# One inference step of an attention and convolution hybrid: SP's transfers in the attention in the kernel's order, and conv sums dealt later

## The chip, the cores and the metric

The kernel runs on one core of a Trainium2 chip. The metric is the device time of one execution in microseconds (us), the median of several runs. Five engines run at the same time, each with its own list of instructions: TensorE (PE, matmuls, with its weight loads shown as PEld), VectorE (DVE), ScalarE (ACT), GpSimd (POOL) and SyncE (SP). SP issues nearly all DMA transfers here. An instruction that waits for another engine or for a transfer holds up whatever stands behind it in the list of its own engine.

## What is computed

One layer of a streaming encoder, for a prompt of 1024 frames and a sample of 32 frames that continues 512 cached ones. The model width is 1024, with 16 heads of 64 channels and a causal depthwise convolution of width 31. The reference, cut to what matters:

```python
def mixer_inputs(x, norm_g, w_in, b_f, q_g, k_g):
    h = rmsnorm(x, norm_g)
    cols = lambda a, w: h @ w_in[:, a:a + w]
    q = rmsnorm(cols(OFF_Q, ATTN_WIDTH).reshape(B, T, N_HEADS, HEAD_DIM), q_g) * (HEAD_DIM ** -0.5)
    k = rmsnorm(cols(OFF_K, ATTN_WIDTH).reshape(B, T, N_HEADS, HEAD_DIM), k_g)
    v = cols(OFF_V, ATTN_WIDTH).reshape(B, T, N_HEADS, HEAD_DIM)
    logf = jax.nn.log_sigmoid((cols(OFF_F, N_HEADS) + b_f).astype(jnp.float32))
    u = cols(OFF_UA, CONV_WIDTH) * jax.nn.sigmoid(cols(OFF_UB, CONV_WIDTH))
    ga, gb, ma, mb = (cols(o, 1024) for o in (OFF_GA, OFF_GB, OFF_MA, OFF_MB))
    return q, k, v, logf, ga, u, gb, ma, mb

def fox_attend(q, k, v, cq, ck, qpos, kpos):
    s = einsum('bqhd,bkhd->bhqk', q, k) + (cq - ck)       # cumulative log forget gates
    p = softmax(where(qpos >= kpos, s, min))
    return einsum('bhqk,bkhd->bqhd', p, v)

def mixer_outputs(x, o_attn, conv, ga, gb, ma, mb, ln_g, ln_b, w_pa, w_pb, w_out):
    ya = (o_attn * silu(ga)) @ w_pa
    yb = (silu(layernorm(conv, ln_g, ln_b)) * silu(gb)) @ w_pb
    return x + (sigmoid(ma) * ya + sigmoid(mb) * yb) @ w_out
```

All products are made in float32 accuracy: a weight and an activation are each split into a high and a low part, and three matmuls (high by high, low by high, high by low) stand for one.

## The kernel before

**Stages.** By the trace: the inputs are transposed and the first convolution input is made (to about 55 us); u and v projections follow (to about 210); then q and k, two feature blocks of 128 channels at a time, with the convolution's taps on DVE (to about 530); the gate ga (to about 580); the attention (to about 1087); and the closing projections pa, pb and out.

**A projection** (`steps`) takes one 128-channel feature block: one `raw` weight tile of 512 KB is loaded (L109), ACT reads it once for its scale (`junk`, L117) and makes the high part (`wh`, L138), DVE makes the low part (`wl`, L141), and PE goes over three chunks of 352 columns, each of eight steps of three matmuls (L183). A finished chunk is read out of PSUM by ACT (`t`, L926) and stored by SP (`s_gb` and the like, L927).

**The attention** has 16 heads of 8 query blocks and four blocks of sample heads. The list `seq` holds them in order; iteration n of the main loop does this:

```python
start(seq[n + 3])                                   # scores of a block, L1087 and L1088
if getattr(seq[n + 5], "i", 1) == 0:
    seq[n + 5].head.load()                          # eight transfers, L942 to L949
b.turn()                                            # transposes of block n, L1112
fill(4)                                             # 12 matmuls of a gate projection, L183
seq[n - 2].values()                                 # for block 7: 40 matmuls po, L1131
heads[...].load_v()                                 # V of the next head, L956
```

`head.load()` brings QB, KB, QA and KA of one head, six pieces of 256 KB and two of 16 KB, 1568 KB in all. The first scores matmul (L1087) reads KB and QB, the second (L1088) KA and QA. The pool `hp` has two buffers of each, so one head can be read while another is loaded. The gate projections gb, ma and mb serve as filler: `fill(4)` takes four steps of them, half a chunk, so a chunk spans two iterations. The filler's PSUM comes from one bank (`pq`). The output of a pair of heads is stored from `ot` (L1140) after two steps on DVE (L1136, L1138).

**What sets the order.** A scheduler orders each engine's instructions ahead of the run. In the attention PE is taken out of it (`tc.manual_schedule(engines={E.PE})`): PE runs in the order in which the kernel is written. SP, DVE, ACT and POOL are ordered by the scheduler, so that a transfer written late in the program can stand early in SP's list.

**Convolution.** `conv_taps(f)` puts 31 taps of filter f in the list `taps`: the first is an ACT instruction that makes y (L361), the others are DVE instructions (L364). `beat`, called once for each projection step, deals them out at the rate of the stage. After the taps follow `from_shift` and `into_sums` (L341 to L347), which add y to `mean` on DVE, square y on ACT (L342) and add the squares to `rstd` on POOL (L347). `later(n, fn)` calls fn n steps later. In the q/k stage POOL also makes the low part of squares for the norm statistics (`sql`, L863), which PE multiplies (`pst`, L871). `u_tile` clears the first 30 columns of a convolution input (L388).

Of the kernel before, what the change touches and what calls it, by code (L numbers as in the profile page):

```python
# [8 lines left out]
F32 = mybir.dt.float32  # L9
# [4 lines left out]
AF = mybir.ActivationFunctionType  # L14
# [15 lines left out]
CW = T + 30 + TS  # L30
# [23 lines left out]
def build(tc, xT, xt, wv, wf, ckT, cv, clT, stT, vec, cst, yT, kT, vO, lfO, cpT, csT):  # L54
    nc = tc.nc
# [3 lines left out]
    def pool(name, bufs=1, stack=es, **kw):  # L59
        return stack.enter_context(tc.tile_pool(name=name, bufs=bufs, reuse_waits="tile", **kw))  # L60
# [19 lines left out]
    rstd = lnp.tile([128, TT], F32, name="rstd")  # L80
# [108 lines left out]
    late = []  # L189
# [3 lines left out]
    def later(n, fn):  # L193

        pace["n"] += 1
        late.append((pace["tick"] + n, pace["n"], fn))
        late.sort(key=lambda e: e[:2])
# [82 lines left out]
    class Banks:  # L280

        n = 0
# [11 lines left out]
    cvp = pool("cvp", 2, stack=pcv)  # L294
    us = {}
    taps = []
    pend = []

    def pump(n):
        for _ in range(min(n, len(taps))):  # L300
            taps.pop(0)()

    PCS = ((0, T, 0), (T + 30, TS, T))
    sides = {}
# [22 lines left out]
    def kept(f, y):  # L327
        nc.sync.dma_start(s_y[f, :, :T], y[:, :T])
        nc.sync.dma_start(s_y[f, :, T:], y[:, T + 30:])
# [6 lines left out]
    def into_sums(f, y):  # L336
        for o, n, a in PCS:
            if f == 0:
                nc.vector.tensor_copy(mean[:, a:a + n], y[:, o:o + n])
            else:  # L340
                nc.vector.tensor_add(mean[:, a:a + n], mean[:, a:a + n], y[:, o:o + n])  # L341
        nc.scalar.activation(y, y, AF.Square)  # L342
        for o, n, a in PCS:
            if f == 0:
                nc.gpsimd.tensor_copy(rstd[:, a:a + n], y[:, o:o + n])
            else:
                nc.gpsimd.tensor_add(rstd[:, a:a + n], rstd[:, a:a + n], y[:, o:o + n])  # L347
        if f == 7:
            sides["ready"] = True

    def sums(f):
        return [lambda: from_shift(f, sides["y", f]), lambda: into_sums(f, sides["y", f])]

    def conv_taps(f):
        u = us.pop(f)

        def tap(i):
            w = vec_t[:, V_WDW + f * KC + i:V_WDW + f * KC + i + 1]
            if i == 0:
                y = sides["y", f] = (u7p if f > 5 else cvp).tile([128, CW], F32, name="y", tag="y", bufs=2)  # L360
                nc.scalar.activation(y, u[:, 0:CW], AF.Identity, bias=vcol(V_BDW, f), scale=w)  # L361
                return 0.1
            y = sides["y", f]
            t = nc.vector.scalar_tensor_tensor(y, u[:, i:i + CW], w, y, op0=ALU.mult, op1=ALU.add)  # L364
            if f > 5:
                tc.keep_in_program_order(t)
            if i == KC - 1:
                kept(f, y)

        items = [lambda i=i: tap(i) for i in range(KC)]  # L370
        if f == 7:
            taps.extend(pend + items)
            pend.clear()
        else:
            taps.extend(items[:4] + pend + items[4:])
            pend[:] = sums(f) if f else []

    def pieces(o, n):
# [5 lines left out]
    def u_tile(f):  # L384
        if f > 3:
            pump(len(taps) - 97)
        u = us[f] = (u7p if f > 5 else cvp).tile([128, UW], F32, name="u", tag="u", bufs=2 if f > 5 else 4)
        nc.gpsimd.memset(u[:, 0:30], 0.0)  # L388
        nc.sync.dma_start(u[:, 30 + T:60 + T], stT[f])
        return u  # L390

    def u_done(f):
        u = us[f]
        nc.sync.dma_start(cpT[f], u[:, T:T + 30])
        nc.sync.dma_start(csT[f], u[:, 62 + T:62 + T + 30])
        conv_taps(f)

    def u_steps(f, pj):
        u = u_tile(f)

        def ev_ub(c, sl, ps, inv):
            for a, b in pieces(c * CH, CH):
                nc.scalar.mul(u[:, b], ps[:, a], inv)
            if c == 2:
                for b in (slice(30, 30 + T), slice(60 + T, 60 + T + TS)):
                    sides["sigmoid"] = nc.scalar.activation(u[:, b], u[:, b], AF.Sigmoid)

        def ev_ua(c, sl, ps, inv):
            for a, b in pieces(c * CH, CH):
                nc.vector.scalar_tensor_tensor(u[:, b], ps[:, a], inv, u[:, b], op0=ALU.mult, op1=ALU.mult)  # L410

        for g, ev in (("ub", ev_ub), ("ua", ev_ua)):
            for _ in steps((g, f), X, XL, pj, ev):
                yield
        u_done(f)

    def u_proj(*a, **k):
        for _ in u_steps(*a, **k):
            pass
# [14 lines left out]
    E = mybir.EngineType  # L434
# [40 lines left out]
    def vcol(base, f):  # L475
        return vec_t[:, base + f:base + f + 1]
# [64 lines left out]
    def x_split(c, ws, u, jobs):  # L541
# [21 lines left out]
        for kt in range(KT):  # L563
# [12 lines left out]
            drain((2, 5 if c == 0 else 2))  # L576

    u0 = u_tile(0)
    ua0 = xip.tile([128, TT], F32, name="ua0")
    ws0 = [[xip.tile([128, KT, 128], F16, name=a, tag=a, bufs=2) for a in ("wh0", "wl0")] for _ in range(2)]  # L580
# [96 lines left out]
    u7p = pool("u7p", 1, stack=p2, side="right")  # L677
# [52 lines left out]
    for c in range(4):  # L730
# [16 lines left out]
        for t in range(8):  # L747
            ps = pj.tile([128, 512], F32, name="pjv", tag="pj")
            n = 0
# [148 lines left out]
    def tables_again(last="sigmoid"):  # L898

        t = nc.scalar.preload_act_table_set(LNEXP)  # L900
        tc.add_manual_dep(t.ins, sides[last].ins.name,
                          mybir.DependencyInfo(mybir.DependencyClass.NoSync, mybir.DependencyReason.DATA),
                          reason="tables behind another's")
        sides["tables"] = t
# [52 lines left out]

    pace["rate"] = R_U
    u_proj(7, pj)
    assert not late  # L960
    pqk.close()
    pv.close()
    hp = pool("hp", 2, stack=p2, side="right")
# [6 lines left out]
            pass  # L970
    tables_again("silu")
    pump(len(taps) - (2 * KC - 2))
    order.close()
    pcv.close()
    pps.close()


    pe = ExitStack()
    pe.enter_context(tc.manual_schedule(engines={E.PE}))
    pace["rate"], pace["credit"] = R_A, 0.0  # L980
    taps.extend(sums(7))
    psS = pool("psS", 2, stack=p2, space=PS)
# [242 lines left out]
    for _ in flow:  # L1225
        pass
    p2.close()


    p3 = ExitStack()  # L1230
# [5 lines left out]
    class Banks3:  # L1236
        n = 0
# [383 lines left out]
```

## Time and profile before

| what | value |
|---|---|
| time, median of 3 runs | 1381.76 us (1381.34 to 1382.31) |
| time of the profiled execution | 1380.92 us |
| its span | 1379.1 us, mean granted clock of PE 0.988 |
| PE busy | 1327.1 us, 96% of the span, 9383 matmuls |
| DVE busy | 969.3 us, 70% |
| ACT busy | 722.4 us, 52% |
| POOL busy | 501.1 us, 36% |
| share of the chain of waits that ended last | PE 78%, DVE 7%, DMA 5%, ACT 4%, issue 4% |
| transferred | 194.96 MB, mean 141 GB/s |

The busy time of an engine is the time in which it worked; the span is from the first to the last instruction. The chain of waits is followed back from the last instruction to what released each step. "Issue" is time in which an engine waited for nothing that the profile shows. In rows of SP's queue (SPq) the duration is that of the issue, not of the transfer. A wait row reads: engine, line, what it waited for, total us, times, longest us.

### The profile page before, as it was taken

To read this page: it belongs to the slowest core of one execution; us is meant where nothing else is said; L and a number is where in the kernel's file an instruction comes from. 1 tells how busy PE (TensorE), PEld (TensorE's weight loads), DVE (VectorE), ACT (ScalarE), POOL (GpSimd) and SP (SyncE) were. 2 spreads that over 40 slices of the span, in tenths; PEclk is the share of its full clock that TensorE was granted. 3 is DMA by queue.
4 is the path that set the end of the run, shared out by engine and by line. 5 is a ranking of instruction groups with operands and counts; after the bars stand their busy time and mean duration, and the time that the engine had idled before them with its cause. 6 is when DMAs were issued, how large, how long until landed. Compare 5 with 4: busy or idle time off the path is not lost.

```text
span 1379.1 us, 24809 instructions
## 1 busy us (share of the span) xinstructions
PE 1327.1 (96%) x9383; PEld 1008.5 (73%) x9383; DVE 969.3 (70%) x1524; ACT 722.4 (52%) x1362; POOL 501.1 (36%) x556
## 2 busy tenths in 40 slices
PE   8999999999999999979889999989899999999999
PEld 5577876665666666657667667767676699999998
DVE  5797879777888888877768767645554479265664
ACT  6644555756676743555555556555554466333320
POOL 1101015445385820233423332222222239355553
PEclk8999999999999999999999999999999999999999
DMA  6333243429252533434445446544432498634462
GB/s 245 95 129 109 91 110 119 130 88 269 68 190 70 180 100 122 148 104 113 140 127 158 115 139 173 139 114 136 137 96 74 160 334 261 205 121 140 143 196 68
DMA packets 113496, 194.96 MB, mean 141 GB/s; under 512 B 34081, under 2 KB 80033, under 8 KB 113377
## 3 DMA queue, kind: packets, MB, share of 16 engines
q1 hardware_dynamic: 113232, 193.31, 45.8%
q8 instruction: 74, 1.21, 0.4%
q14 instruction: 46, 0.37, 0.1%
q10 hardware_dynamic: 144, 0.07, 0.0%
HBM read 127.68 MB, written 65.64 MB: 140 GB/s over the span
## 4 chain that ended last, share of the span: by engine, by line
PE 78%; DVE 7%; DMA 5%; ACT 4%; issue 4%; POOL 1%; SPq 1%; ACTq 0%; DVEq 0%; POOLq 0%
PE pj L183 53%; PE pjv L754 6%; PE pj L1453 5%; PE po L1131 5%; DMA raw<-wf 4%; PE ptr L1112 3%; PE psS L1087 2%; PE psS L1088 2%; DVE y L364 2%; DVE nm L1092 2%; DVE wl L141 1%; ACT P L1095 1%; ACT t L926 1%; PE pst L871 1%; POOL sql L863 1%
## 5 line engine op out<-in xcount | busy, mean ns | idle before, releaser
L183 PE MATMUL pj<-xh,wh 128*128 128x352 f16 (+2 forms) x1536 | 485.4, 316 | 18.7 <-ACT t L926 18.1
L183 PE MATMUL pj<-xl,wh 128*128 128x352 f16 (+2 forms) x1536 | 484.9, 316 | 0.5
L183 PE MATMUL pj<-xh,wl 128*128 128x352 f16 (+2 forms) x1536 | 484.8, 316 | 0.0
L183 PEld LDWEIGHTS <-wh 128*128 128x128 f16 x3072 | 303.2, 99 | 162.4 <-issue 3.7
L364 DVE SCALAR_TENSOR_TENSOR y<-u,vec_t,y 128x1086 f32<-128x1086 f32 x240 | 341.8, 1424 | 17.3 <-ACT y L361 14.4
L1098 POOL TENSOR_SCALAR P<-P,nm 128x128 f32<-128x128 f32 (+7 forms) x128 | 124.1, 971 | 269.8 <-DVE nm L1097 239.3
L183 PEld LDWEIGHTS <-wl 128*128 128x128 f16 x1536 | 151.7, 99 | 93.4 <-issue 22.8
L141 DVE SCALAR_TENSOR_TENSOR wl<-raw,sc,wh 128x384 f16<-128x384 f32 (+1 forms) x192 | 117.4, 647 | 30.1 <-ACT wh L138 30.0
L1095 ACT ACTIVATE P<-psS,nm 128x128 f32<-128x128 f32 (+7 forms) x128 | 94.7, 740 | 74.3 <-DVE nm L1092 64.3
L1092 DVE TENSOR_REDUCE nm<-psS 128x1 f32<-128x128 f32 (+7 forms) x128 | 96.3, 754 | 7.1
L1115 ACT COPY pt<-ptr 128x512 f32<-128x512 f32 (+3 forms) x128 | 64.3, 502 | 59.3 <-PE ptr L1112 58.6
L1087 PE MATMUL psS<-KB,QB 128*128 128x256 f32 (+2 forms) x192 | 82.8, 432 | 11.4 <-ACT P L1095 11.3
L175 POOL TENSOR_TENSOR wl<-raw,wh 128x384 fp32r<-128x384 f32 (+1 forms) x51 | 63.1, 1264 | 73.9 <-ACT wh L172 58.0
L1112 PE MATMUL ptr<-ident,P 128*128 128x128 f32 x576 | 85.5, 275 | 0.0
L117 ACT ACTIVATE junk<-raw 128x1024 bf16<-128x1024 f32 x62 | 65.2, 1051 | 32.6 <-DMA raw<-wf 32.5
L863 POOL TENSOR_TENSOR sql<-sqf,sqh 128x352 fp32r<-128x352 f32 x48 | 61.6, 1284 | 54.6 <-ACT sqh L860 54.6
L138 ACT ACTIVATE wh<-raw,sc 128x1024 f16<-128x1024 f32 (+1 forms) x68 | 72.4, 1089 | 8.6 <-DVE sc L158 8.2
L1112 PEld LDWEIGHTS ptr<-ident,P 128*128 128x128 f32 x576 | 70.3, 142 | 5.8
L1131 PE MATMUL po<-pt,V 128*64 128x256 f32 x640 | 72.6, 382 | 1.3 <-ACT pt L1115 1.3
L1097 DVE RECIPROCAL nm<-nm 128x1 f32<-128x1 f32 x128 | 20.5, 160 | 73.8 <-ACT P L1095 72.8
L1090 DVE TENSOR_TENSOR psS<-psS,cmask 128x128 f32<-128x128 f32 x128 | 37.5, 294 | 49.2 <-PE psS L1088 48.4
L754 PE MATMUL pjv<-vwh,xh 128*128 128x260 f16 x256 | 70.1, 274 | 0.0
(271 smaller groups left out, 2584.7 us busy)
## 6 DMA issues: line engine op xcount, KB each, us to landing
raw<-wf SPq DMA_DIRECT2D x92, 512.0 KB
QB<-s_q SPq DMA_DIRECT2D x32, 256.0 KB
KB<-s_k SPq DMA_DIRECT2D x32, 256.0 KB
kT<-qn SPq DMA_DIRECT2D x8, 528.0 KB
s_ga<-t SPq DMA_DIRECT2D x24, 176.0 KB
s_gb<-t SPq DMA_DIRECT2D x24, 176.0 KB
s_ma<-t SPq DMA_DIRECT2D x24, 176.0 KB
s_mb<-t SPq DMA_DIRECT2D x24, 176.0 KB
```

Of the source, the lines that this page charges most:

```text
L138: nc.scalar.mul(wh[:, ks, :], raw[:, ks, :], self.s[:, i:i + 1])
L141: nc.vector.scalar_tensor_tensor(wl[:, ks, :], raw[:, ks, :], self.s[:, i:i + 1], wh[:, ks, :], op0=ALU.mult, op1=ALU.subtract)
L183: nc.tensor.matmul(ps, a[:, kt, :], b(kt, sl), start=(first and n == 0), stop=(last and n == N - 1))
L364: t = nc.vector.scalar_tensor_tensor(y, u[:, i:i + CW], w, y, op0=ALU.mult, op1=ALU.add)
L754: nc.tensor.matmul(ps[:, :VC], a, b, start=(n == 0), stop=(n == 23))
L863: nc.gpsimd.tensor_sub(sql, sqf, f32(sqh))
L1087: nc.tensor.matmul(ps[:, b, :wm], QB[:, qsl], KB[:, ksl], start=True, stop=False)
L1092: nc.vector.tensor_reduce(nm[:, 0:1], ps[:, :nb, :w], axis=AX.XY, op=ALU.max, negate=True)
L1095: nc.scalar.activation(P[:, :nk].rearrange("p (b w) -> p b w", b=nb), ps[:, :nb, :w], AF.Exp, bias=nm[:, 0:1], accum_out=nm[:, 1:2])
L1098: nc.gpsimd.tensor_scalar(P[:, :nk], P[:, :nk], nm[:, 2:3], 1.0, op0=ALU.mult, op1=ALU.mult)
L1112: nc.tensor.transpose(pt[:, 128 * j:128 * j + 128], P[:, 128 * (4 * u + j):128 * (4 * u + j) + 128], ident)
L1131: nc.tensor.matmul(po[rows], V[:, j, :], parts[c][:, j, :], start=(c % 2 == 0 and j < 2), stop=(c % 2 == 1 and j >= 2 * c))
```

## The change

Five edits. In the attention SP joins PE in `manual_schedule`, so that SP issues its transfers in the order in which the kernel is written; behind the attention's loop that region ends and a new one with PE alone begins. In `into_sums` the square is dealt 9 steps later and the additions on POOL 13 steps later. The first tap of filters 0 to 5 is put five places before the end of the list of the taps that still stand, y gets a third buffer there, and the pending sums follow three taps instead of four. The clearing of u goes from POOL to DVE. What is still due in `late` is done at the end of the ga stage, where before it had to be empty ahead of it.

```diff
-        nc.scalar.activation(y, y, AF.Square)
-        for o, n, a in PCS:
-            if f == 0:
-                nc.gpsimd.tensor_copy(rstd[:, a:a + n], y[:, o:o + n])
-            else:
-                nc.gpsimd.tensor_add(rstd[:, a:a + n], rstd[:, a:a + n], y[:, o:o + n])
-        if f == 7:
-            sides["ready"] = True
+
+        def added():
+            for o, n, a in PCS:
+                if f == 0:
+                    nc.gpsimd.tensor_copy(rstd[:, a:a + n], y[:, o:o + n])
+                else:
+                    nc.gpsimd.tensor_add(rstd[:, a:a + n], rstd[:, a:a + n], y[:, o:o + n])
+            if f == 7:
+                sides["ready"] = True
+
+        later(9, lambda: nc.scalar.activation(y, y, AF.Square))
+        later(13, added)
...
-                y = sides["y", f] = (u7p if f > 5 else cvp).tile([128, CW], F32, name="y", tag="y", bufs=2)
+                y = sides["y", f] = (u7p if f > 5 else cvp).tile([128, CW], F32, name="y", tag="y", bufs=2 if f > 5 else 3)
...
         items = [lambda i=i: tap(i) for i in range(KC)]
+        if f < 6:
+            taps.insert(max(0, len(taps) - 5), items.pop(0))
...
-            taps.extend(items[:4] + pend + items[4:])
+            taps.extend(items[:3] + pend + items[3:])
...
-        nc.gpsimd.memset(u[:, 0:30], 0.0)
+        nc.vector.memset(u[:, 0:30], 0.0)
...
-    assert not late
...
+    while late:
+        late.pop(0)[2]()
...
-    pe.enter_context(tc.manual_schedule(engines={E.PE}))
+    pe.enter_context(tc.manual_schedule(engines={E.PE, E.SP}))
...
+    pe.close()
+    pe = ExitStack()
+    pe.enter_context(tc.manual_schedule(engines={E.PE}))
```

Line numbers of the changed kernel are larger by 6 from the conv edits on, and by 7 from the attention's loop on.

**SP early in the attention, before.** The list of SP around the loads of heads 2 (`QB_7326` to `KA_7327`) and 3 (`QB_7677` and on); `t_...` are the chunks of a gate projection in the order in which they are made.

```order
L946 DMA QA_7325<-s_q_57 64x1024
L947 DMA QA_7325<-s_aq_61 4x1024
L927 DMA s_gb_67<-t_7066 128x352
L948 DMA KA_7327<-s_k_58 64x1024
L949 DMA KA_7327<-s_ak_62 4x1024
L109 DMA raw_7423<-wf 128x1024
L109 DMA raw_7513<-wf 128x1024
L927 DMA s_gb_67<-t_7143 128x352
L927 DMA s_gb_67<-t_7212 128x352
L1009 DMA vc_7690<-cv 128x4x256
L956 DMA V_7276<-s_v_59 128x8x64
L927 DMA s_gb_67<-t_7310 128x352
```

The loads of head 2 stand ahead of three stores of the filler, two raw tiles directly behind them.

**The same place in the change.**

```order
L933 DMA s_gb_67<-t_7143 128x352
L933 DMA s_gb_67<-t_7212 128x352
L962 DMA V_7276<-s_v_59 128x8x64
L933 DMA s_gb_67<-t_7310 128x352
L948 DMA QB_7326<-s_q_57 64x1024
L949 DMA QB_7326<-s_q_57 64x1024
L950 DMA KB_7328<-s_k_58 64x1024
L951 DMA KB_7328<-s_k_58 64x1024
L952 DMA QA_7325<-s_q_57 64x1024
L953 DMA QA_7325<-s_aq_61 4x1024
L954 DMA KA_7327<-s_k_58 64x1024
L955 DMA KA_7327<-s_ak_62 4x1024
```

Head 2's eight loads now follow the stores of three chunks (t_7143, t_7212, t_7310) that they preceded; the raw tiles have moved behind the next stores, one at a time. PE's list is the same but for a few matmuls of the layernorm's sums.

**SP at head 5 of the change**, where the store of a pair's output and V stand ahead of the loads.

```order
L1127 DMA ga_8282<-s_ga_66 128x1024
L933 DMA s_gb_67<-t_8347 128x352
L1147 DMA s_o_70<-ot_7398 128x1024
L962 DMA V_8379<-s_v_59 128x8x64
L948 DMA QB_8427<-s_q_57 64x1024
L949 DMA QB_8427<-s_q_57 64x1024
L950 DMA KB_8429<-s_k_58 64x1024
```

In the list of before, the same `QB_8427` stood ahead of the store of chunk `t_8203`, several stores earlier.

## The prediction

> **What bounds the kernel now.** I read the busy shares first, then the time by stage, then PE's waits in the stage that the change touches, then SP's queue there.
>
> ```profile
> PE 1327.1 (96%) x9383; PEld 1008.5 (73%) x9383; DVE 969.3 (70%) x1524; ACT 722.4 (52%) x1362; POOL 501.1 (36%) x556
> 1087.00:1379.00 292.00, 288.06 (x1976) 279.64 (x1972) 176.74 (x227) 111.40 (x149) 149.69 (x120) 1.00 0.58 188
> 580.00:1087.00 507.00, 473.90 (x3463) 341.18 (x3463) 324.17 (x699) 273.11 (x589) 148.66 (x216) 0.98 0.45 124
> 210.00:530.00 320.00, 313.62 (x2073) 205.87 (x2072) 263.47 (x320) 205.88 (x369) 169.08 (x160) 0.99 0.43 134
> ```
>
> The first row is busy time, share and instructions. The others hold start and end, length, then the busy time of PE, its weight loads, DVE, ACT and POOL, the granted clock, the DMA share and GB/s. PE sets the end everywhere. After the attention (second row) it is solid, and nothing there can be won or lost by this change. In the attention (580 to 1087) PE is idle for 33 us, and a clock of 0.98 over 507 us costs some 8 to 10 us more. In the q/k stage (210 to 530) 6 us are idle. So a change of order gains at most some 50 us in all, while a PE that begins to wait loses without such a limit.
>
> ```profile
> PE pj L183 <- ACT t L926: 17.5, 17, 4.2
> PE psS L1087 <- ACT P L1095: 9.5, 5, 5.0
> ACT junk L117 <- DMA raw<-wf: 30.1, 14, 4.6
> 615.91 0.69 PE L1087 MATMUL psS<-KB,QB 128*128 128x384 f32 x1 [4.96 <-ACT P L1095]
> 607.15 0.50 SPq L949 DMA_DIRECT2D KA<-s_ak  x1
> 607.75 6.14 DMA raw<-wf
> ```
>
> These are waits in the attention (total, times, longest), one PE instruction with the idle time before it, one issue on SP, and one piece of the chain of waits. PE waits for ACT, ACT stands at a weight load that has not landed: at 615.91 the long stall is a raw tile issued at 607.75 that takes 6.14 us. It was issued directly behind the last (607.15) of a head's eight loads.
>
> ```profile
> 631.20 0.44 PE L1087 MATMUL psS<-KB,QB 128*128 128x384 f32 x1
> 634.02 0.48 PE L1087 MATMUL psS<-KB,QB 128*128 128x448 f32 x1
> 635.44 0.33 SPq L927 DMA_DIRECT2D s_gb<-t  x1
> 638.14 0.47 SPq L942 DMA_DIRECT2D QB<-s_q  x1
> 640.40 0.40 PE L1087 MATMUL psS<-KB,QB 128*128 128x256 f32 x1
> 640.64 0.28 PE L1088 MATMUL psS<-KA,QA 68*128 68x256 f32 x1
> SPq L942 <- PE psS L1088: 42.0, 13, 6.5
> SPq L927 <- ACT t L926: 115.0, 30, 8.9
> ```
>
> Here are PE's and SP's timeline around one change of head, and two of SP's own waits. At 640.40 PE starts block 0 of head 2; the QB that SP issues at 638.14 is already head 3's, one head ahead. SP waits in its queue 42.0 us for the old head's last scores and 115.0 us for results to store, and nobody pays, since loads are a whole head early.
>
> **The change: SP in the program's order.** In program order a head's loads (L942 to L949) stand behind the scores of the iteration that begins at S = 634.02, and block 0 of that very head comes two iterations later: KB and QB are used 640.40 - 634.02 = 6.4 us after S, KA and QA 6.6 us after S. So the lead shrinks from a head to two iterations, for all 15 heads after the first. What else SP must do first is what stands ahead of QB in its queue, and how long the loads take is in these rows:
>
> ```profile
> 735.01 0.45 SPq L942 DMA_DIRECT2D QB<-s_q  x1
> 737.29 0.59 SPq L945 DMA_DIRECT2D KB<-s_k  x1
> 739.10 0.45 SPq L948 DMA_DIRECT2D KA<-s_k  x1
> 739.58 0.48 SPq L949 DMA_DIRECT2D KA<-s_ak  x1
> 739.10 5.31 DMA KA<-s_k
> 765.09 4.15 DMA KB<-s_k
> DMA packets 788, 2.00 MB, mean 200 GB/s; under 512 B 138, under 2 KB 385, under 8 KB 787
> ```
>
> The loads were issued from 735.01, the last large one landed at 739.10 + 5.31 = 744.41, 9.4 us after the first issue, and a last small one is issued 0.48 us later; I take 9.65. That is 1568 KB, and the window from 735 to 745 moves 2.00 MB at 200 GB/s, so it is close to what the queue gives here.
>
> Head by head, by the new SP order:
> - Eight heads (1, 2, 3, 8, 12 to 15) have a store of a gate chunk ahead of QB, whose matmuls end only at S. By the rows at 635.44 the store leaves at S + 1.4 and takes 0.33, so QB leaves at S + 1.75, KA and QA are there at S + 11.4, and PE waits 11.4 - 6.6 = 4.8 us. 8 x 4.8 = 38.
> - Four heads (5, 7, 9, 11) have the store of a head pair's output and V ahead instead.
>
> ```profile
> 654.58 4.47 PE po L1131 x40
> 659.09 0.37 SPq L956 DMA_DIRECT2D V<-s_v  x1
> 665.72 0.32 SPq L1140 DMA_DIRECT2D s_o<-ot  x1
> ```
>
> The matmuls of the output end at 659.05, which is one iteration ahead of S (2.8 us, as from 631.20 to 634.02), and the store left 6.7 us after them. If it is ready before S, QB leaves 0.7 us after S at the latest and the wait is 0.7 + 9.65 - 6.6 = 3.7; if it takes 6.7 us again, 7.6. DVE made it late in the row at 665.72 behind other work, so I stay nearer the low end: 5. 4 x 5 = 20.
> - Three heads (4, 6, 10) have only stores whose chunk ended an iteration earlier: QB leaves at S, the wait is 3.0. Together 9.
>
> That is 67 us of new waiting. The other loads (V, ga, the sample's) stand where they have several iterations to land, and I cost them at nothing; without that cover the four samples would pay about the 2.0 us that PE now waits at one of them at worst, 8 in all.
>
> **The clock behind each wait.**
>
> ```profile
> 808.14 0.31 PE L183 MATMUL pj<-xh,wh 128*128 128x352 f16 x1 [2.15 <-ACT t L926]
> 807.40:810.90 3.50, 2.76 (x13) 1.77 (x13) 3.34 (x8) 1.47 (x5) 1.32 (x1) 0.74 0.14 52
> 810.90:812.50 1.60, 1.60 (x7) 0.66 (x6) 1.25 (x4) 1.16 (x3) 1.03 (x1) 0.50 0.00 0
> 618.00:621.40 3.40, 3.40 (x14) 1.93 (x14) 2.08 (x4) 1.06 (x3) 1.81 (x2) 0.50 0.00 0
> 621.40:625.00 3.60, 3.60 (x25) 2.76 (x24) 1.66 (x4) 1.53 (x4) 0.52 (x2) 1.00 0.02 5
> ```
>
> After the 2.15 us of idle at 808.14 the granted clock falls to 0.50 until 812.50, and after the 5 us at 615.91 a whole stretch of 3.4 us runs at 0.50 and then at 1.00 again. A stretch of 3.4 us at half speed loses 1.7 us. I count it for 14 of the 15 heads: 24 us. The Trainium skill, "TensorE: Matmul & The Clock Gate", section on the HAM clock gate, has the clock fall only after an idle window of about 3.4 us; the row at 808.14 differs, with 2.15 us of idle. By the skill's figure the 24 us would shrink to little, which is the second rival below.
>
> **What the same edit gives back.** In the new order a raw tile's load no longer stands in a pair behind a head's eight, and with PE waiting at each head ACT catches up. I take all of the 17.5 + 9.5 = 27 us of PE's waits for ACT above as gone, and the 8 us of low clock behind them. Between nothing and 37 us, I take 35, near the top, because 30.1 us of ACT's waits are for raw alone.
>
> **The conv edits.** In the q/k stage the square and the additions of a conv sum block others:
>
> ```profile
> 327.20 2.84 POOL L347 TENSOR_TENSOR rstd<-rstd,y 128x1024 f32<-128x1024 f32 x2 [2.40 <-ACT y L342]
> 330.98 0.46 PE L871 MATMUL pst<-sql,bones 128*128 128x352 f32 x1 [2.43 <-POOL sql L863]
> PE pst L871 <- POOL sql L863: 5.9, 4, 2.4
> L388 POOL MEMSET u<- x8: 123/123/124, 0.9 to 188.6; 128x30 f32 x8
> ```
>
> POOL stands 2.40 us at its addition for ACT's square, then works 2.84 us, and PE's statistics matmul at 330.98 waits 2.43 us for the product queued behind. Dealt some steps later, the addition finds its input ready: I take 2.4 us plus 1.7 of clock and a little of the rest, 5 us gained. The bound above is all 5.9 and twice the clock, 9; the bound below, that the 2.84 us of addition now hit another product at each of seven filters, is 7 x 2.4 = 17 lost. Eight clearings of 0.12 us moved from POOL to DVE, the third y buffer and the drained rest lie beside PE's work: nothing, at most 1 us.
>
> **The sum**: 67 + 24 - 35 - 5 = +51 on the profiled 1380.92, hence 1432; the median of the runs shown is 0.8 us higher than that execution: **1433 us**.
>
> **Rivals.**
> - *The clock holds.* Each head's wait is split in two: KB's last half is issued 2.3 us after QB (735.01, 737.29) and lands some 4.15 to 5.3 us later, at S + 8.2 to 9.3, so the first scores matmul (L1087) runs between two idle pieces of 1.8 to 2.9 us each. For it: neither piece is as long as the 4.96 at 615.91. Against it: 2.15 at 808.14. Then 67 - 40 = +27: 1409.
> - *Raw tiles late too.* SP reaches the raw loads only behind stores that wait for PE, and ACT stands at them again. Before, 14 such waits; if eight of them cost PE the 4.96 of the row at 615.91, +40 on the forecast: 1473. Against it: PE's waits at heads delay the need as well.
> - *The loads are early enough (faster).* With nothing ahead of QB, eight issues take 4.1 us to KA, which lands 4.15 after its issue if the transfers do not press on each other: S + 8.2, a wait of 1.6 us per head, without a fall of the clock. 15 x 1.6 = 24 against 40 won: -16, 1366. It decides when the mean wait of a head is under 40 / 15 = 2.7 us with the clock kept. Against it: the 9.4 us measured at 735.01 and the store ahead of QB in eight heads.
>
> **How the numbers follow.** Forecast 0.67, clock holds 0.16, raw late 0.11, early enough 0.05, all terms cancelling 0.01. The first three are slower by over 0.2% (about 2.8 us, what a measurement of this kernel tells from no change): 0.94; faster 0.05; same 0.01. The forecast's own range from the bounds of the heads behind an output store, of the returned 35 and of the conv edits is 1415 to 1460; the lower end is drawn down to 1400 to take in the second case, the upper to 1465.
>
> **What would show it.** Right: at block 0 of each head PE idle of 3 to 8 us, at L1087 and L1088 with the DMA of KB or KA as releaser; half clock behind most of them; QB's issue two iterations, not nine, ahead of its use; no 5 us raw stall at 611; the stage after the attention still 292 us. Wrong: no idle at the first blocks, or the attention no longer than 507 us; idle at other blocks released by raw or ACT would speak for the third case.

## The result, and the profile after

The changed kernel takes 1449.75 us (median of 4 runs, 1443.85 to 1454.04) against 1381.55 us before: a ratio of 1.0494, with a 95% interval of 1.0451 to 1.0537, or 68 us slower. The profiled execution is the shortest of the four (1443.85 us).

The stages of the changed kernel first: start and end, length, busy time of PE, weight loads, DVE, ACT and POOL, granted clock, DMA share, GB/s. The attention now runs from about 575 to 1150.

```profile
580.00:1155.00 575.00, 498.55 (x3461) 354.20 (x3461) 324.30 (x694) 275.59 (x588) 144.24 (x218) 0.93 0.42 114
1155.00:1442.00 287.00, 282.53 (x1936) 275.97 (x1934) 175.65 (x225) 108.93 (x146) 146.46 (x118) 1.00 0.59 191
```

Both attention windows hold nearly the same matmuls (3461 here, 3463 before), so two numbers can be set side by side. PE's idle time there is 575 - 498.6 = 76.4 us, against 33.1 before: 43 us more. PE's busy time for the same work is 498.6 us against 473.9: 25 us more, at a granted clock of 0.93 in place of 0.98. Together 68 us. The profiled execution as a whole is only 63 us longer than that of before, since it reaches the attention 6 us sooner; that the medians also differ by 68 us is chance. The last stage runs at full clock as it did.

What PE waited for in the changed kernel's attention (total us, times, longest):

```profile
PE psS L1094 <- DMA KB<-s_k: 31.8, 11, 5.7
PE psS L1095 <- DMA KA<-s_ak: 28.3, 12, 2.8
PE psS L1095 <- DMA KA<-s_k: 4.2, 2, 2.3
PE pj L183 <- ACT t L932: 4.1, 8, 1.0
PE psS L1094 <- issue: 2.5, 1, 2.5
PE psS L1094 <- ACT P L1102: 2.4, 3, 1.3
```

And what ACT waited for there:

```profile
ACT pt L1122 <- PE ptr L1119: 140.4, 82, 8.8
...
ACT junk L117 <- DMA raw<-wf: 9.0, 9, 2.4
```

Of PE's rows the first three were not there before: 64 us of waiting for a head's loads. The row "issue" stands for a wait of 2.5 us whose releaser the profile does not name; it lies at the first scores matmul of head 14, so it is most likely one more of these. In exchange PE's two largest waits for ACT (17.5 and 9.5 us before) have shrunk to 4.1 and 2.4, and ACT stands 9.0 us at raw tiles, not 30.1. It now waits for PE instead: 140.4 us at `pt`, where it was 57.6 before.

One change of head (to head 2) on PE's timeline, where the bracket holds the idle time before an instruction:

```profile
628.88 0.48 PE L1094 MATMUL psS<-KB,QB 128*128 128x448 f32 x1
...
637.86 0.36 PE L1094 MATMUL psS<-KB,QB 128*128 128x256 f32 x1 [2.32 <-DMA KB<-s_k]
640.39 0.55 PE L1095 MATMUL psS<-KA,QA 68*128 68x256 f32 x1 [2.17 <-DMA KA<-s_ak]
```

On SP's:

```profile
630.30 0.32 SPq L933 DMA_DIRECT2D s_gb<-t  x1
630.67 0.46 SPq L948 DMA_DIRECT2D QB<-s_q  x1
...
634.75 0.48 SPq L955 DMA_DIRECT2D KA<-s_ak  x1
```

And in the chain of waits:

```profile
634.75 5.50 DMA KA<-s_ak
```

QB leaves at 630.67, behind a chunk's store at 630.30, 1.8 us after the iteration that begins at 628.88. The last piece lands at 634.75 + 5.50 = 640.25, and PE has waited 2.32 us for KB and 2.17 us for KA.

The change to head 3 shows the clock behind such a wait. PE's timeline:

```profile
674.07 0.55 PE L1094 MATMUL psS<-KB,QB 128*128 128x256 f32 x1 [3.64 <-DMA KB<-s_k]
676.93 0.55 PE L1095 MATMUL psS<-KA,QA 68*128 68x256 f32 x1 [2.31 <-DMA KA<-s_ak]
```

The windows around it, in the columns of the stages, with one behind head 2's wait on top:

```profile
639.20:642.60 3.40, 2.21 (x9) 1.90 (x10) 0.93 (x3) 0.77 (x3) 0.00 (x0) 0.60 0.53 198
673.50:677.00 3.50, 0.62 (x2) 0.39 (x2) 0.00 (x0) 0.65 (x2) 0.00 (x0) 0.58 1.02 251
677.00:680.50 3.50, 3.50 (x14) 2.55 (x15) 1.24 (x5) 0.94 (x3) 1.49 (x2) 0.50 0.88 244
680.50:684.00 3.50, 3.50 (x34) 2.09 (x32) 1.15 (x3) 0.58 (x1) 0.42 (x1) 0.95 0.00 1
```

At head 3 PE is idle for 3.64 and 2.31 us; the clock is at 0.58 while it waits and at 0.50 for the 3.5 us after. In this stretch PE gets 14 matmuls through, in the next, at 0.95, it gets 34; they are not all of one shape, so the counts alone are no measure of the clock.

### The profile page after: what moved, and what is told of

Same layout as the page of the kernel before. It is cut to its first block, busy times and chain, and to the rows that moved or that the text cites. A ratio compares the mean times of both kernels' runs of the same rounds, so it can differ in the third digit from the quotient of the medians.

```text
span 1442.0 us, 24764 instructions
## 1 busy us (share of the span) xinstructions
PE 1345.7 (93%) x9383; PEld 1019.0 (71%) x9383; DVE 976.6 (68%) x1532; ACT 724.2 (50%) x1362; POOL 496.6 (34%) x548
## 4 chain that ended last, share of the span: by engine, by line
PE 71%; DMA 11%; DVE 5%; SPq 4%; ACT 4%; issue 3%; POOL 2%; ACTq 0%; POOLq 0%; DVEq 0%
PE pj L183 47%; PE pjv L760 6%; DMA KA<-s_ak 5%; PE pj L1463 5%; PE po L1138 5%; PE ptr L1119 3%; PE psS L1095 1%; DVE y L368 1%; DMA raw<-wf 1%; DMA KA<-s_k 1%; PE psS L1094 1%; DMA a<-s_o 1%; DVE nm L1099 1%; ACT t L932 1%; ACT P L1102 1%
## 5 line engine op out<-in xcount | busy, mean ns | idle before, releaser
L1105 POOL TENSOR_SCALAR P<-P,nm 128x128 f32<-128x128 f32 (+7 forms) x128 | 119.5, 935 | 334.9 <-DVE nm L1104 294.3
L141 DVE SCALAR_TENSOR_TENSOR wl<-raw,sc,wh 128x384 f16<-128x384 f32 (+1 forms) x192 | 120.7, 664 | 31.5 <-ACT wh L138 31.4
L1094 PE MATMUL psS<-KB,QB 128*128 128x256 f32 (+2 forms) x192 | 82.3, 430 | 37.0 <-DMA KB<-s_k 31.8
L1097 DVE TENSOR_TENSOR psS<-psS,cmask 128x128 f32<-128x128 f32 x128 | 37.7, 296 | 115.9 <-PE psS L1095 115.3
L1095 PE MATMUL psS<-KA,QA 68*128 68x256 f32 (+2 forms) x192 | 70.0, 366 | 32.4 <-DMA KA<-s_ak 28.3
L1119 PE MATMUL ptr<-ident,P 128*128 128x128 f32 x576 | 93.6, 294 | 0.9 <-ACT pt L1122 0.9
L1119 PEld LDWEIGHTS ptr<-ident,P 128*128 128x128 f32 x576 | 77.1, 153 | 6.6 <-ACT pt L1122 1.1
L1094 PEld LDWEIGHTS psS<-KB,QB 128*128 128x128 f32 x192 | 37.1, 193 | 54.5 <-issue 34.1
L120 POOL CAST topb<-tops 128x2 bf16<-128x2 f32 x35 | 13.7, 390 | 167.4 <-ACT junk L117 117.3
```

What stands on the lines that cost most here:

```text
L141: nc.vector.scalar_tensor_tensor(wl[:, ks, :], raw[:, ks, :], self.s[:, i:i + 1], wh[:, ks, :], op0=ALU.mult, op1=ALU.subtract)
L1094: nc.tensor.matmul(ps[:, b, :wm], QB[:, qsl], KB[:, ksl], start=True, stop=False)
L1095: nc.tensor.matmul(ps[:, b, :wm], QA[:, qsl], KA[:, ksl], start=False, stop=True)
L1105: nc.gpsimd.tensor_scalar(P[:, :nk], P[:, :nk], nm[:, 2:3], 1.0, op0=ALU.mult, op1=ALU.mult)
L1119: nc.tensor.transpose(pt[:, 128 * j:128 * j + 128], P[:, 128 * (4 * u + j):128 * (4 * u + j) + 128], ident)
```

## The experiments

All but `later_off` were timed several times, each beside the kernel before; ratios are to that kernel, with a 95% interval. Line numbers shift by a few from kernel to kernel; the names of the tiles stay.

**Which part of the change costs the time: the conv edits alone, and SP's order alone.** First the changed kernel with SP given back to the scheduler:

```diff
-    pe.enter_context(tc.manual_schedule(engines={E.PE, E.SP}))
+    pe.enter_context(tc.manual_schedule(engines={E.PE}))
```

> The changed kernel with the scheduler ordering SP in the attention again (PE alone taken out of it), so only the conv edits and the clearing on DVE are left. Theory (the head loads in SP's program order cost all of the loss, the conv edits gain a little in the q/k stage): about 5 us below the kernel before, 1376, the gain between 290 and 350 us of the trace, the attention within 3 us of before. Rival (the conv edits also disturb the attention's DVE and ACT order and carry part of the loss): above 1385.

Then the kernel before with the opposite edit and nothing else:

```diff
-    pe.enter_context(tc.manual_schedule(engines={E.PE}))
+    pe.enter_context(tc.manual_schedule(engines={E.PE, E.SP}))
...
     p2.close()
+    pe.close()
+    pe = ExitStack()
+    pe.enter_context(tc.manual_schedule(engines={E.PE}))
```

> The kernel before with SP in program order in the attention and nothing else. Theory: the whole loss and 5 us more than the changed kernel, 1452 to 1456, PE waiting 60 to 68 us for QB, KB, QA and KA at the first blocks of 15 heads. Rival (the loss needs both edits): 1381 to 1430.

`conv_only` took 1379.32 us, a ratio of 0.9998 (0.9988 to 1.0008), and `sp_only` 1453.33 us, 1.0527 (1.0509 to 1.0544). So SP's order carries the whole loss. `sp_only` came out as expected, with 68 us of waits for loads; `conv_only` is 3 us above the 1376 expected. In the profile of `conv_only` the stretch from 290 to 350 us runs at a clock of 1.00:

```profile
290.00:350.00 60.00, 56.05 (x370) 36.58 (x369) 45.17 (x56) 42.64 (x77) 39.33 (x37) 1.00 0.66 196
```

In the kernel before it was 0.94:

```profile
290.00:350.00 60.00, 55.15 (x343) 35.21 (x342) 42.06 (x52) 40.65 (x76) 35.16 (x37) 0.94 0.67 196
```

That is 370 matmuls in place of 343 in the same time. Compared matmul by matmul, PE is 4.0 us further at the end of that stage, but the medians show no gain; the profiled execution gave back 1.2 us of it by the end, and runs of the kernel before spread over 7 us, so a gain of this size is not seen in them. The pair `sp_only` and changed kernel, whose ratios differ by 0.0033, would fit a gain of about 5 us, but their intervals overlap. That the conv edits shorten the whole kernel is thus not shown.

**Which conv edit gains the 4 us.** `conv_only` with the square and additions issued at once:

```diff
-        later(9, lambda: nc.scalar.activation(y, y, AF.Square))
-        later(13, added)
+        nc.scalar.activation(y, y, AF.Square)
+        added()
```

> conv_only with the square and the additions of a conv sum issued at once again, as in the kernel before; the early first tap, the third buffer, the split of the taps and the clearing on DVE stay. Theory (the 4 us gained between 290 and 350 us of the trace come from dealing these later): that stretch is again within 1 us of the kernel before. Rival (they come from the first tap or the clearing): the 4 us stay.

It was run once: 1376.57 us. Between the matmuls that the kernel before runs at 293 and at 436 us it gained 1.0 us on that kernel, where `conv_only` gained 4.0, and part of the low clock is back (0.97, where the kernel before has 0.94):

```profile
290.00:350.00 60.00, 54.17 (x350) 35.19 (x348) 42.09 (x53) 41.62 (x77) 38.87 (x37) 0.97 0.66 196
```

So most of the 4 us, about 3, come from dealing the sum later, as the first theory had it. The split is rough. Between the same matmuls the runs below that have all conv edits gain 3.1 to 4.8 us on that one execution of the kernel before, and `sp_only` and `before_junk`, which have none, lose 1.4. The total of a single execution is no evidence either way.

**Loads earlier in the program.** The changed kernel with a head's loads one iteration earlier (`lead6`), and three (`lead8`):

```diff
-        if n + 5 < len(seq) and getattr(seq[n + 5], "i", 1) == 0:
-            seq[n + 5].head.load()
+        if n + 6 < len(seq) and getattr(seq[n + 6], "i", 1) == 0:
+            seq[n + 6].head.load()
```

> The changed kernel with a head's loads one iteration earlier in the program (three iterations ahead of use in place of two). Theory: the eight heads behind a chunk's store now stand ahead of it and have 9.4 us, so their wait all but ends (0.3 us); the three heads of the third kind now stand behind a store and wait 2.0 us; the four heads behind the output store of a pair gain nothing, since that store is late however early the load stands behind it, and wait 4 to 7.6 us still. PE's waits for loads fall from 64 to about 28 us, the time to about 1397. Rival (the transfers are slow for want of DMA bandwidth, not late): the waits fall by the 2.8 us of one iteration at every kind of head alike, the four heads too.

> The changed kernel with a head's loads three iterations earlier (five ahead of use). Theory: all loads land in time, PE's waits for them and the low clock behind them end: 1450 - 64 - 25 = 1361; with the 27 us of waits for ACT behind raw tiles not back, since raw loads stand one at a time. Rival (raw waits come back once the head waits are gone): PE waits 20 us and more for ACT again, 1376 to 1385. Rival (the loads compete with the filler's raw tiles wherever they stand): PE waits of over 1 us at most first blocks remain, over 1400.

`lead6` took 1424.27 us (1.0321, 1.0305 to 1.0336), 27 us above what was expected, and PE still waits 37.7 us for loads (and 3.6 us at the first scores matmul of head 15, with no releaser named):

```profile
PE psS L1094 <- DMA KB<-s_k: 16.0, 6, 3.6
PE psS L1095 <- DMA KA<-s_ak: 15.8, 8, 2.6
PE psS L1095 <- DMA KA<-s_k: 5.9, 4, 1.9
```

One change of head there, on PE:

```profile
657.22 0.44 PE L1094 MATMUL psS<-KB,QB 128*128 128x384 f32 x1
...
669.65 0.35 PE L1094 MATMUL psS<-KB,QB 128*128 128x256 f32 x1 [3.02 <-DMA KB<-s_k]
671.93 0.55 PE L1095 MATMUL psS<-KA,QA 68*128 68x256 f32 x1 [1.92 <-DMA KA<-s_ak]
```

And on SP:

```profile
659.72 0.32 SPq L1147 DMA_DIRECT2D s_o<-ot  x1
660.13 0.39 SPq L962 DMA_DIRECT2D V<-s_v  x1
660.57 1.04 SPq L948 DMA_DIRECT2D QB<-s_q  x1
```

The loads stand behind the scores at 657.22 in the program, but QB leaves only at 660.57, since the output store ahead of it waits for DVE until 659.72. The expectation counted four heads behind such a store; in `lead6` all seven odd heads after head 1 stand behind one. Heads 2, 6, 10 and 14 stand right behind V, which waits for the output's matmuls, and at the head shown the last piece of the loads is used at 671.93, 11.4 us after QB's issue, where 9.65 had been taken. The rival, by which every kind of head gains alike, falls too: against the changed kernel heads 1, 8 and 12 wait 3.6 to 4.6 us less each, the seven behind an output store 0 to 2 us less.

`lead8` took 1376.23 us (0.9961, 0.9945 to 0.9976): no wait for a head's loads is left, and what came back is what the first rival said. PE's largest wait in its attention:

```profile
PE pj L183 <- ACT t L932: 22.5, 20, 4.5
```

ACT's wait for raw tiles:

```profile
ACT junk L117 <- DMA raw<-wf: 32.2, 17, 7.1
```

SP, and ACT behind it:

```profile
683.00 0.48 SPq L955 DMA_DIRECT2D KA<-s_ak  x1
683.53 0.37 SPq L109 DMA_DIRECT2D raw<-wf  x1
```

```profile
690.97 1.06 ACT L117 ACTIVATE junk<-raw 128x1024 bf16<-128x1024 f32 x1 [4.85 <-DMA raw<-wf]
```

PE waits 22.5 us for ACT again, and ACT waits 32.2 us for raw tiles; `lead8_junk` below tells how much of the first comes from the second. Here a raw tile is issued at 683.53, again just behind a head's loads, and ACT stands 4.85 us until it is there. So the small waits for raw in the changed kernel were no merit of SP's order: there ACT had been held up by PE instead.

**What stands ahead of the loads in SP's queue.** `lead6` with the output store and the load of V put behind the head's loads:

```diff
-                nc.sync.dma_start(s_o[self.head.h // 2, :, :T], ot)
+                held.append(lambda h=self.head.h: nc.sync.dma_start(s_o[h // 2, :, :T], ot))
...
             seq[n + 6].head.load()
+        while held:
+            held.pop(0)()
...
-            heads[seq[n - 2].head.h + 1].load_v()
+            held.append(heads[seq[n - 2].head.h + 1].load_v)
```

> The kernel with the loads three iterations ahead (lead6), and the store of a pair's output and the load of V, which in the program stand just ahead of a head's loads, put just behind them. Theory (in lead6 QB left 3.4 us after the iteration's start in the seven heads behind an output store, and 0.5 us in those behind V, since these two wait for PE's output matmuls): QB leaves at the iteration's start in all, the first wait in the seven heads ends, what is left is what the transfers take beyond 9.4 us: 1 to 1.5 us a head. PE's waits for loads fall from 38 to about 15 us, the time from 1424 to about 1393. Rival (the transfers' duration under contention decides, whatever stands ahead): waits stay above 28 us, the time above 1412.

It took 1371.64 us (0.9933, 0.9908 to 0.9957), faster than either theory gave. One wait of 0.6 us for loads is left:

```profile
PE psS L1095 <- DMA KA<-s_k: 0.6, 1, 0.6
```

At the change to head 3, SP and then PE:

```profile
645.60 0.32 SPq L933 DMA_DIRECT2D s_gb<-t  x1
646.02 0.45 SPq L948 DMA_DIRECT2D QB<-s_q  x1
```

```profile
651.98 0.44 PE L1094 MATMUL psS<-KB,QB 128*128 128x384 f32 x1
```

The theory was right in kind and too small in size. QB now leaves at 646.02, 6 us before the scores (651.98) behind which it stands in the program. SP does not wait for PE at that place; it waits only where an instruction of its own must, here at the store of a chunk at 645.60. With the two late ones out of the way the loads leave as soon as the store ahead of them. Moving two transfers in the queue gave 53 us on top of the 25 that moving the loads by one iteration had given. With the loads two iterations ahead, as in the changed kernel, these two transfers were not moved, so what that alone would give is not known.

**The clock by itself.** The changed kernel with PE kept busy, by matmuls whose result nobody reads, where it would wait for loads:

```diff
+                if i == 0 and self.head.h:
+                    dm = psT.tile([128, 512], F32, name="ptr2", tag="T")
+                    for _ in range(15):
+                        nc.tensor.matmul(dm[:, :CH], xh[:, 0, 0:128], xh[:, 0, 0:CH], start=True, stop=True)
                 nc.tensor.matmul(ps[:, b, :wm], QB[:, qsl], KB[:, ksl], start=True, stop=False)
+                if i == 0 and self.head.h:
+                    for _ in range(14):
+                        nc.tensor.matmul(dm[:, :CH], xh[:, 0, 0:128], xh[:, 0, 0:CH], start=True, stop=True)
```

> The changed kernel with 15 matmuls of no use ahead of the first scores matmul of each head's block 0, and 14 between it and the second, 4.3 us at full clock, so that PE works in the time in which it waited for the loads. Theory (24 us of the loss are low clock behind the idle pieces): PE's waits for loads fall from 64 to 10 to 20 us, the loads land no sooner, and the rest of the work runs at full clock: 1450 - 20 to 25 + about 5 for matmuls that outlast a wait: 1425 to 1435. Rival (the low clock does not come from these waits, or costs nothing because the loads' landing sets the pace anyway): 1448 and above.

```profile
580.00:1150.00 570.00, 546.19 (x3979) 386.72 (x3978) 325.34 (x703) 279.95 (x595) 149.00 (x222) 1.00 0.45 121
```

PE's waits for loads:

```profile
PE psS L1098 <- DMA KB<-s_k: 5.5, 6, 1.5
PE psS L1102 <- DMA KA<-s_ak: 3.1, 7, 0.6
```

And ACT's wait for raw tiles:

```profile
ACT junk L117 <- DMA raw<-wf: 44.7, 18, 7.1
```

1426.31 us (1.033, 1.0307 to 1.0353): 23 us less than the changed kernel, for work that does nothing. The attention's clock is 1.00 (the window takes in some 15 us of the closing stage) and 9 us of waits for these loads are left; the loads stand in SP's order where they stood. So low clock behind the waits costs some 23 us, about the 25 us by which PE's busy time had grown. The size is rough: between the two profiled executions, the shortest of the changed kernel and the longest of `warm`, it is 15 us, and some of the added matmuls outlast the wait that they fill (they take 70 us, and with them and the 9 us left PE spends 79 us where it waited 67). ACT's waits for raw are at 44.7 us with SP's order unchanged, so that order does not make them small. Only 7.3 us of waits for a chunk's read-out by ACT reach PE here.

**The waits for raw tiles.** What was left in `lead8` and was there before the change: ACT's first pass over a raw tile. The scheduler draws it forward. Counted in exponentials on ACT, it stands mostly 7 to 9 ahead of where the hold puts it in `lead8`, and mostly 15 to 20 in the kernel before; why the scheduler chose that place is not shown. Held behind the exponential that precedes it in the program (here on `lead8`):

```diff
-            nc.scalar.activation(junk[:, :raw.shape[1] * raw.shape[2]], raw.rearrange("p a b -> p (a b)"),
-                                 AF.Square, accum_out=self.tops[:, i:i + 1])
+            with tc.issue_after(sides["exp"].ins) if "exp" in sides else ExitStack():
+                nc.scalar.activation(junk[:, :raw.shape[1] * raw.shape[2]], raw.rearrange("p a b -> p (a b)"),
+                                     AF.Square, accum_out=self.tops[:, i:i + 1])
...
-                nc.scalar.activation(P[:, :nk].rearrange("p (b w) -> p b w", b=nb), ps[:, :nb, :w], AF.Exp,
-                                     bias=nm[:, 0:1], accum_out=nm[:, 1:2])
+                sides["exp"] = nc.scalar.activation(P[:, :nk].rearrange("p (b w) -> p b w", b=nb), ps[:, :nb, :w],
+                                                    AF.Exp, bias=nm[:, 0:1], accum_out=nm[:, 1:2])
```

> The kernel with the loads five iterations ahead, and ACT's reading pass over a raw tile (junk) held behind the softmax exponential that precedes it in the program; the scheduler had drawn it some eight blocks forward, to where the raw tile had hardly landed. Theory (what is left of PE's idle time there is ACT standing at raw tiles): ACT's 32 us of waits for raw go to under 5, PE's 22.5 us of waits for ACT to under 8, with the clock behind them about 25 us less: 1350. Rival (PE then waits for the scale or for the high and low parts, which come later): 1370 and above, with PE waiting at tot or at the first chunk of a weight.

The same hold on the kernel before, and on `lead6_defer`:

> The kernel before, SP ordered by the scheduler as it was, with only ACT's reading pass over a raw tile held behind the softmax exponential that precedes it in the program. Theory (the time to be won in the attention is ACT standing at raw tiles, and SP's order has nothing to do with it): ACT's 30 us of waits for raw go to under 6, PE's idle time in the attention falls by 20 us, the clock behind it by 6 to 8: 1352 to 1358. Rival (the gain of lead8_junk needs SP in program order, because the scheduler issues raw tiles directly behind a head's loads and lands them too late for the pass even so): 1368 and above, with ACT still waiting over 12 us for raw.

> lead6_defer with the same hold on ACT's reading pass. Theory (in lead6_defer the head loads wait no longer, and what is left is ACT at raw tiles, 25.9 us there): 1350 to 1358, as lead8_junk. Rival (with ACT ahead of raw gone, loads three iterations ahead are late again, since PE runs faster): PE waits over 8 us for loads, 1365 and above.

`lead8_junk` took 1358.13 us (0.9834, 0.9809 to 0.986), `defer_junk` 1357.9 us (0.9825, 0.9793 to 0.9856), `before_junk` 1364.2 us (0.9868, 0.9829 to 0.9907). PE's waits for ACT and for loads in `before_junk`:

```profile
PE pj L184 <- ACT t L927: 10.9, 16, 1.3
PE psS L1088 <- ACT P L1096: 3.3, 3, 2.5
PE psS L1088 <- DMA QB<-s_q: 2.6, 1, 2.6
```

No wait of `junk` for a raw tile is left in the attention of any of the three, and they beat both kernels of this study. The hold needs no change of SP's order: on the kernel before, whose list of SP stays nearly as it was (434 of the 440 transfers from 560 us on in the same sequence, as many raw tiles, 12, close behind a head's loads), it gives 17 us. So the waits for raw came from the place of ACT's pass, and the place of the raw tiles in SP's queue could stay. The gain is short of the 24 to 30 us expected, since PE still waits 10.9 us for ACT's read-out of chunks, which these waits had been taken to contain. In `lead8_junk` too PE's wait for chunks falls only by half, from 22.5 to 11.9 us, and the time is 8 us above the 1350 expected. Why these waits remain was not tried. The other two have medians 6 us lower than `before_junk`, with intervals that overlap; in the profiled executions that difference is there when the attention starts (6.2 and 6.5 us), so it is not SP's order in the attention that brings it.

## Why the prediction was right

The forecast was 1433 us, 51 slower; the time was 1449.75, 68 slower, inside the range, and the mechanism was the one foretold. Point by point:

- **Waits for a head's loads: 67 us foretold, 64 measured** (31.8 + 28.3 + 4.2), or 67 with the 2.5 us at head 14. By the three kinds of heads 38, 20 and 9 us were foretold, and PE's waits add up to 40, 23 and 4. That the total fits so well is in part luck, since two errors nearly cancelled. The loads mostly take longer than the 9.65 us assumed: at head 2 the last piece landed 9.6 us after QB's issue, at head 3 11.4 us (665.44 to 676.79). The 200 GB/s taken as close to what the queue gives is not its limit either, since 247 were moved around head 3. But at the heads without a late store QB does not wait for the iteration: at head 6, costed as leaving at S with a wait of 3.0 us, it left 2.3 us before S (771.28), and PE waited 1.4 us. SP's timeline, the chain of waits and PE's timeline of the changed kernel have it:

```profile
665.44 0.50 SPq L948 DMA_DIRECT2D QB<-s_q  x1
...
769.00 0.58 SPq L948 DMA_DIRECT2D QB<-s_q  x1
```

```profile
669.62 7.17 DMA KA<-s_ak
```

```profile
771.28 0.49 PE L1094 MATMUL psS<-KB,QB 128*128 128x448 f32 x1
...
779.38 0.36 PE L1095 MATMUL psS<-KA,QA 68*128 68x256 f32 x1 [1.37 <-DMA KA<-s_ak]
```

The output store stood ahead of heads 3, 13 and 15 too, with V and a chunk's store between, which the sorting of heads into kinds had missed; it cost nothing, as QB left there at S + 1.6 to 1.9 all the same. The other loads (V, ga, the samples'), costed at nothing, are not in PE's list of waits. The samples' may still have cost something: at heads 3, 7, 11 and 15 six of them are issued right behind the eight loads, and KA is used 11.4 to 14.1 us after QB's issue, at the other heads where PE waited for loads 9.7 to 11.3. No run moved them, so this stays open.
- **The clock: the term that was too small.** Foretold were 24 us of new low clock less 8 us that would end, 16 in all, from one stretch of 3.4 us for each of 14 heads. Measured are 25 us net. The clock fell at 13 heads, at ten of them for two such stretches, one partly in the wait itself, as from 673.5 to 680.5 above. The 23 us that `warm` won are of the same size. Head 2's idle pieces of 2.32 and 2.17 us were enough for a clock of 0.60 behind them. The Trainium skill, "TensorE: Matmul & The Clock Gate", section on the HAM clock gate, wants some 3.4 us of idle time for that; this trace disagrees, with 2.32 and 2.17 us and a matmul between.
- **What comes back: 27 us of waits for ACT foretold, about 20 measured** (17.5 + 9.5 before, 4.1 + 2.4 after). The reason given was half right: PE's waits let ACT catch up. That raw tiles are early enough in program order was wrong: `lead8` has 32.2 us of waits for raw again. Nor do the raw tiles explain all of the 27 us: `before_junk` has no wait for them and keeps 10.9 + 3.3.
- **The q/k stage: 5 us foretold, 4.6 measured** in the profiled execution up to the attention's start, and by `later_off` mostly through the sums dealt later. At the end of the kernel it is not seen: `conv_only` has a ratio of 0.9998.
- **The rivals.** "The clock holds" fell with the 0.93 of the attention. "Raw tiles late too" fell in the changed kernel (9.0 us of waits). "The loads are early enough" fell with the 64 us; `lead6_defer` shows the point from which it would have decided, with waits of 0.6 us and a time below that of before.

Of the 17 us between forecast and measurement, 12 lie in the profiled executions: 9 of clock (25 for 16) and 3 of idle time in the attention (43 for 67 - 27); 1 us by which the first 60 us of the kernel ran shorter is made up by small differences elsewhere. The other 5 come from the medians: that of the changed kernel lies 5.9 us above its profiled execution, and that of before, as the forecast had it, 0.8.

The range came out, but not from its stated parts. The bounds of the heads behind an output store (15 to 30 us), of what is given back (0 to 37) and of the conv edits (9 gained to 17 lost) add up to 1422 to 1500, not to 1415 to 1460.

## What to carry to other kernels

A queue kept in program order releases a transfer not when the program reaches it but when the last waiting transfer ahead of it goes; so look for late stores ahead of early loads, and not only at where the loads stand. Here the waits on PE cost over a third more through the clock behind them (25 us on 64), and even matmuls of no use won 23 us back. When one wait disappears after a change, look whether another engine had only become later: it comes back when that one is mended.

## What the runs showed of the hardware

- In the changed kernel's attention the granted clock fell at the 13 heads where PE waited 2.3 to 7.5 us, mostly in two pieces split by a matmul, for one or two stretches of 3.4 us. It did not fall at head 6, with a single wait of 1.37 us, nor at head 4, with 1.26 us. The record of the granted clock has 23 stretches at half speed in the changed kernel's attention, 5 before, and none with the added matmuls.
- The same eight loads of 1568 KB took 9.6 us at head 2 and 11.4 at head 3, where six transfers for a sample were issued right behind them and the window from 665 to 677 us moved 2.96 MB (that these transfers slowed the loads is not shown):

```profile
DMA packets 2156, 2.96 MB, mean 247 GB/s; under 512 B 1190, under 2 KB 1449, under 8 KB 2155
```
